# A decoder layer on one Trainium2 core: a fifth seven-product pair in three of the four down-projection passes

## The chip, the core and the metric

The kernel runs on one core of one Trainium2 chip. The core has TensorE (PE, matrix products into PSUM banks of 128 x 512 float32), VectorE (DVE), ScalarE (ACT), GpSimd (POOL) and SyncE (SP, which here only issues DMAs). In the profile PEld is TensorE's weight load. The metric is the device time of one launch in microseconds (us), as the median of the timed runs. Changes within about 0.2% of it cannot be told from no change.

## The reference

One decoder layer: 256 tokens, model width 2048, feed-forward width 5632, all in float32. The part that the change touches is the channel mixer:

```python
h = rmsnorm(x, pre_ffn_g[l])
u = causal_dwconv(h @ w_up[l], conv_w[l], conv_b[l])
gate, val = jnp.split(u, 2, axis=-1)
y = (jax.nn.gelu(gate, approximate=True) * val) @ w_down[l]
x = x + rmsnorm(y, post_ffn_g[l])
```

Ahead of it stand the input projection, two attention groups and the output projection, which stay as they are.

## The kernel before

**Numbers.** A float32 weight tile is split in two parts: ACT copies it to float32r (the high part), DVE subtracts that from the raw values (the low part). A product then is three matmuls: high by high, high by low, low by high (`product`, L963).

**The stages.** The up-projection runs over 22 pairs of 128-channel tiles of gate and value, 11 in each of two halves (`for g`, L1058). For each pair PE makes gate and value, DVE, POOL and ACT do the convolution, the activation and the product, and the result, already transposed, is split into two `G` tiles (channel x token, high and low). After each half the down-projection takes that half's 22 `G` tiles as contraction and runs twice over `w_down`: once for output columns 0 to 1023, once for 1024 to 2047 (`for n in (0, 2)`, L1102). So there are four passes, two per half. Results add up in `y_sb`.

**Eight products or seven.** A pass takes the `G` tiles by pairs `u` (tiles 2u and 2u+1). With the 256 tokens as two blocks, the pair's two tiles as two blocks, and the 1024 columns as two blocks, a pair is a 2x2 block product: eight block products of three matmuls each, 24 matmuls of 512 columns. For the pairs in `FAST` (0, 2, 4, 6) it is done with seven products, 21 matmuls, by sums of blocks: four sums of `G` blocks, made once per half by `token_sums` (L951) and kept split in the tile `sums`, and four differences of weight blocks, made in each pass by DVE (L1007 to L1014) into the tile `tb` and then split like weights. A fast pair thus has ACT and DVE split one 512-column block (`b11`) and three of 1024 (`f13`, `f24`, `b2`), besides the four differences; an ordinary pair splits two of 1024.

**Banks.** Four "early" banks (`m1, m5, m7, m6`, tag "acc") get only products of fast pairs and are summed into `y_sb` after the last fast pair (`add_early`); four "late" banks (`p2, p3, p4, p22`, tag "att") get the rest of the fast pairs and all ordinary products, and are summed after the pass's last pair (L1144 to L1149). The last pair's products are held and done bank by bank (`block`), so that each late bank can leave while PE fills the next. In the last pass three pairs are held, and the end of the kernel (L1170 on) interleaves their four blocks with the final norm.

**Places.** Raw weights, 1024 columns at a time (512 KB), are loaded by SP into eight rotating places: five `raw` tiles, two in `extra`, one in `tb`. Split weights have five pairs of places (`whi`, `wlo`); the last pass keeps its last pair's splits in `rest`. A place is loaded or written again once its last reader is through.

**Order.** PE's instructions stand in the order in which they are written. The other engines' are ordered by a scheduler, which takes a ready instruction by its place in the program; at the end of the kernel, from L1179, they too stand as written. In the first pass of a half the pairs run 1, 3, 0, 5, 2, 7, 4, 8, 6, 9, 10, in the second from 0 to 10.

## Time and profile before

| | |
|---|---|
| timed runs | 1065.41, 1064.84, 1065.19 us; median 1065.19 us |
| profiled execution | 1064.31 us, of which the span of its instructions is 1062.6 us |
| DVE busy in the span | 839.7 us |
| ACT, POOL busy in the span | 639.1 us, 229.3 us |
| DMA read and written | 201.68 MB, 4.21 MB |
| the four passes begin (first matmul) | 580.42, 637.5, 936.94, 994.06 us |

A row of a group names line, engine, operation and tiles, then shapes; "x" is the count. In a table by windows the columns are the window, its length, the busy time (and count) of PE, PEld, DVE, ACT and POOL, the granted TensorE clock, the DMA share and GB/s. A row of a timeline begins with start and duration; in brackets stands the idle time before it and what ended it. A line of waits names who waited for whom: total us, times, longest. Durations overlap: a matmul's row is longer than its distance to the next.

### The profile page before, as it was taken

The page shows a single profiled execution, that of the slowest core. Times are in us where ns is not written, and L with a number is a line of the kernel's source. Part 1 is how long each engine was busy: PE and PEld are TensorE (multiplying, and loading weights), DVE is VectorE, ACT ScalarE, POOL GpSimd, SP SyncE. Part 2 cuts the span into 40 slices and gives each one's busy share as a digit, 9 for nine tenths or more (in the row PEclk, how much of TensorE's full clock was granted, in tenths as well). Part 3 has the DMA queues.
Part 4 walks back from the last instruction along what each step waited for, and adds up shares of the span by engine and source line. Part 5 has one row for each costly group of instructions (what it writes and reads, how often), then busy time and mean ns, then how long its engine had stood idle before and what let it go on. Part 6 is the DMA issues. An engine that isn't in the chain of part 4 may idle for free.

```text
span 1062.6 us, 16272 instructions
## 1 busy us (share of the span) xinstructions
PE 1049.6 (99%) x5890; PEld 914.6 (86%) x5890; DVE 839.7 (79%) x1369; ACT 639.1 (60%) x1096; POOL 229.3 (22%) x256
## 2 busy tenths in 40 slices
PE   9999999999999999999999999999999999999996
PEld 7889988888889888888888888888888888888885
DVE  5988887887467887787767999668778687789987
ACT  6767667776556765566655556446556565556551
POOL 4253335441022121211212000002121121200004
PEclk9999999999999999999999999999999999999998
DMA  8745566555773876656665666666566665656563
GB/s 280 217 120 168 162 209 202 165 170 162 282 236 107 280 231 187 193 180 185 211 188 188 193 204 206 213 196 190 169 209 188 197 197 180 194 179 200 194 242 121
DMA packets 154285, 207.08 MB, mean 195 GB/s; under 512 B 6845, under 2 KB 131037, under 8 KB 153181
## 3 DMA queue, kind: packets, MB, share of 16 engines
q1 hardware_dynamic: 153200, 203.37, 60.7%
q10 hardware_dynamic: 1004, 2.68, 0.6%
q8 instruction: 46, 0.75, 0.3%
q14 instruction: 35, 0.28, 0.1%
HBM read 201.68 MB, written 4.21 MB: 194 GB/s over the span
## 4 chain that ended last, share of the span: by engine, by line
PE 84%; DVE 9%; issue 2%; DMA 2%; ACT 2%; POOL 1%; DVEq 0%; SPq 0%; POOLq 0%; ACTq 0%
PE bank_acc L284 15%; PE bank_att L284 14%; PE bank_acc L309 12%; PE bank_att L967 9%; PE bank_acc L290 8%; PE bank_att L290 7%; PE bank_acc L253 7%; DVE wlo L313 4%; PE bank_acc L258 4%; PE bank_acc L967 2%; PE bank_att L475 1%; PE bank_att L510 1%; DVE wlo L115 1%; PE bank_acc L932 1%; DMA raw<-in_w_down_dram 1%
## 5 line engine op out<-in xcount | busy, mean ns | idle before, releaser
L115 DVE TENSOR_TENSOR wlo<-raw,whi 128x1024 fp32r<-128x1024 f32 (+3 forms) x271 | 328.5, 1224 | 127.0 <-ACT whi L112 118.4
L112 ACT CAST whi<-raw 128x1024 fp32r<-128x1024 f32 (+3 forms) x270 | 273.2, 1029 | 131.8 <-issue 88.8
L899 POOL TENSOR_TENSOR room<-room,rowf 128x256 f32<-128x256 f32 x88 | 100.3, 1160 | 393.9 <-DVE room L898 392.0
L284 PE MATMUL bank_acc<-hT,whi 128*128 128x512 f32 x736 | 173.3, 390 | 0.0
L284 PEld LDWEIGHTS bank_acc<-hT,whi 128*128 128x128 f32 x736 | 136.4, 188 | 27.4
L967 PE MATMUL bank_att<-whi,G 128*128 128x512 f32 x488 | 156.0, 389 | 0.0
L284 PE MATMUL bank_att<-hT,whi 128*128 128x512 f32 x640 | 150.6, 390 | 0.0
L284 PEld LDWEIGHTS bank_att<-hT,whi 128*128 128x128 f32 x640 | 118.7, 188 | 23.9
L967 PEld LDWEIGHTS bank_att<-whi,G 128*128 128x128 f32 x488 | 91.6, 188 | 18.9
L967 PE MATMUL bank_att<-wlo,G 128*128 128x512 f32 x244 | 95.0, 389 | 0.2 <-DVE wlo L313 0.2
L290 PEld LDWEIGHTS bank_acc<-hT,wlo 128*128 128x128 f32 x736 | 89.3, 188 | 2.0
L290 PE MATMUL bank_acc<-hT,wlo 128*128 128x256 f32 x736 | 89.8, 279 | 0.0
L901 ACT ACTIVATE room<-room,cw 128x256 f32<-128x256 f32 x88 | 53.0, 602 | 60.6 <-POOL room L899 60.6
L253 PE MATMUL bank_acc<-hT,whi 128*128 128x512 f32 x352 | 88.0, 395 | 0.0
L309 PE MATMUL bank_acc<-whi,oT 128*128 128x512 f32 (+1 forms) x272 | 81.7, 379 | 0.0
L290 PEld LDWEIGHTS bank_att<-hT,wlo 128*128 128x128 f32 x640 | 77.6, 188 | 1.7
L290 PE MATMUL bank_att<-hT,wlo 128*128 128x256 f32 x640 | 77.9, 279 | 0.0
L903 DVE SCALAR_TENSOR_TENSOR room<-room,cw 128x256 f32<-128x256 f32 x88 | 62.4, 709 | 17.6 <-ACT room L901 17.3
L253 PEld LDWEIGHTS bank_acc<-hT,whi 128*128 128x128 f32 x352 | 63.3, 188 | 11.5
L313 DVE TENSOR_TENSOR wlo<-raw,whi 128x1024 fp32r<-128x1024 f32 (+1 forms) x56 | 61.3, 1119 | 12.1 <-ACT whi L312 12.1
L312 ACT CAST whi<-tb 128x1024 fp32r<-128x1024 f32 x42 | 44.0, 1050 | 43.0 <-PE bank_att L967 19.6
L312 ACT CAST whi<-raw 128x1024 fp32r<-128x1024 f32 (+1 forms) x56 | 52.3, 958 | 27.1 <-PE bank_att L967 20.6
(254 smaller groups left out, 1594.0 us busy)
## 6 DMA issues: line engine op xcount, KB each, us to landing
raw<-in_w_up_dram SPq DMA_DIRECT2D x176, 512.0 KB, 4.2
raw<-in_w_down_dram SPq DMA_DIRECT2D x58, 512.0 KB, 4.7
raw<-in_w_in_dram SPq DMA_DIRECT2D x51, 512.0 KB, 4.7
raw<-in_w_out_dram SPq DMA_DIRECT2D x32, 512.0 KB, 4.6
extra<-in_w_down_dram SPq DMA_DIRECT2D x20, 512.0 KB, 4.7
raw<-in_w_in_dram SPq DMA_DIRECT2D x16, 384.0 KB, 3.6
tb<-in_w_down_dram SPq DMA_DIRECT2D x10, 512.0 KB, 3.5
cb<-c_dram SPq DMA_DIRECT2D x8, 256.0 KB, 3.8
```

Source lines behind the costliest of these rows:

```text
L112: i1 = act.copy(hi[:, cs], raw[:, cs])
L115: i2 = dve.tensor_tensor(lo[:, cs], raw[:, cs], hi[:, cs].bitcast(F32), op=ALU.subtract)
L253: pe.matmul(b, parts[u][0][:, a, m * P:(m + 1) * P], hT[:, kt, :], start=(kt == 0), stop=(kt == KT - 1))
L284: pe.matmul(b, parts[u][0][:, a, m * P:(m + 1) * P], hT[:, kt, :], start=(kt == 0), stop=(kt == KT - 1))
L290: pe.matmul(b[:, 256:512], parts[u][1][:, a, m * P:(m + 1) * P], hT[:, kt, 0:256], start=False, stop=False)
L309: pe.matmul(b, a, r[:, cols], start=(first and i == 0), stop=(last and i == 2))
L312: act.copy(hi, src)
L313: dve.tensor_tensor(lo, src, hi.bitcast(F32), op=ALU.subtract)
L899: pool.tensor_tensor(u[:, 2:258], u[:, 2:258], rowf, op=ALU.mult)
L901: act.activation(y, u[:, 2:258], AF.Identity, bias=cw[:, 3, ch:ch + 1], scale=cw[:, 2, ch:ch + 1])
L903: dve.scalar_tensor_tensor(y, u[:, 1:257], cw[:, 1, ch:ch + 1], y, op0=ALU.mult, op1=ALU.add)
L967: pe.matmul(b[:, to] if to else b, a, r[:, cols], start=(first and i == 0), stop=(last and i == 2))
```

## The change

`FAST` gets pair 8. Three of the four passes use all five pairs; the last pass of the second half keeps four. The first pass of a half runs the pairs in the order 1, 3, 0, 5, 2, 7, 4, 6, 9, 8, 10.

`token_sums` keeps three sums for pairs 0 to 6: the fourth (the sum of the blocks a21 and a22) is written over a21 in the activations before they are split into `G`, where nothing else reads a21. Pair 8 keeps four sums, since it is ordinary in the last pass.

The differences of weight blocks are written over the raw weight tiles, in place of `tb`. Raw tiles have six rotating places in the first half (five `raw`, one `extra`) and eight in the second (two more in the memory of `hT`, free after the last up-projection). Split weights have seven rotating places: the five before, two more in the memory of the convolution's room and a tile `slot`. `rest` is gone. The post-norm's gain table lies in the memory of `hT`.

`fast_pass` becomes `column_pass`, which returns three functions: `ahead` (load and split the first pair), `run` and `block`. The second pass's first pair is prepared before the first pass's last sums are written down, and the pair behind the last fast one before the early sums. In a fast pair the seven products are ordered by when their splits are made; in a pass's first fast pair those into late banks come last.

```diff
-FAST = (0, 2, 4, 6)
+FAST = (0, 2, 4, 6, 8)
...
+        def sums_at(i):
+
+            return (i * 768, 3) if i < 4 else (4 * 768, 4)
+
-        def token_sums(into, y0, y1):
+        def token_sums(i, g, sums, y0, y1):
 
             s = fp.tile([P, 4, P], F32, tag="cst", name="s")
+            at, n = sums_at(i)
             a11, a21 = y0[:, 0:P], y0[:, P:256]
             a12, a22 = y1[:, 0:P], y1[:, P:256]
...
+            if n == 4:
+                split(g[0][:, 0:256], g[0][:, 256:512], y0)
+            split(g[1][:, 0:256], g[1][:, 256:512], y1)
+            dve.tensor_tensor(s[:, 0, :], a11, a21, op=ALU.subtract)
+            s1 = s[:, 3, :] if n == 4 else a21
+            dve.tensor_tensor(s1, a21, a22, op=ALU.add)
+            dve.tensor_tensor(s[:, 1, :], s1, a11, op=ALU.subtract)
+            dve.tensor_tensor(s[:, 2, :], a12, s[:, 1, :], op=ALU.subtract)
+            if n == 3:
+                split(g[0][:, 0:256], g[0][:, 256:512], y0)
+            w = n * P
+            split(sums[:, at:at + w], sums[:, at + w:at + 2 * w],
+                  s[:, 0:n, :].rearrange("p k c -> p (k c)"))
...
-        def fast_pass(G, sums, order, k00, c0, load, tb, early, late, add_early, hold=1,
-                      keep=None):
+        def column_pass(G, sums, some, order, k00, c0, load, parts, hold=1):
...
+            def prepare(u):
+                ra, rb = (load(w_rows(w_down, k00 + 2 * u + a, 1, c0, UNIT)) for a in range(2))
+                if u not in some:
+                    return [parts(r, UNIT) for r in (ra, rb)]
+                b11 = parts(ra[:, left], 512)
+                b2 = parts(rb, UNIT)
+                dve.tensor_tensor(ra[:, left], ra[:, right], ra[:, left], op=ALU.subtract)
+                dve.tensor_tensor(ra[:, right], rb[:, right], ra[:, right], op=ALU.subtract)
+                f13 = parts(ra, UNIT)
+                dve.tensor_tensor(rb[:, right], rb[:, right], ra[:, left], op=ALU.subtract)
+                dve.tensor_tensor(rb[:, left], rb[:, left], rb[:, right], op=ALU.subtract)
+                return b11, b2, f13, parts(rb, UNIT)
+
+            def ahead():
+                ready[order[0]] = prepare(order[0])
...
+                steps = [(m1, of(k, 0), b11, left), (p2, of(k + 1, 0), b2, left),
+                         (p3, s_of(2), b2, right), (m5, s_of(3), f13, left),
+                         (m7, s_of(0), f13, right), (m6, s_of(1), f24, right),
+                         (p4, of(k + 1, 1), f24, left)]
+                if u == fast[0]:
+                    steps = steps[0:1] + steps[3:] + steps[1:3]
+                for bk, a, b, cols in steps:
+                    product(bk, *a, b, cols, first(bk), end and bk in (m1, m5, m7, m6))
+
+            def run(add_early):
+                early, late = ([bank(tag) for _ in range(4)] for tag in ("acc", "att"))
+                banks.extend(zip(late, (0, 0, 1, 1), (left, right, left, right)))
+                for i, u in enumerate(order):
+                    forms = ready.pop(u) if u in ready else prepare(u)
+                    if u in some:
+                        seven(u, forms, *early, *late[:3])
+                        if u == fast[-1] and hold == 1:
+                            nxt = order[i + 1]
+                            ready[nxt] = prepare(nxt)
+                            add_early(*early)
...
-            extra = fp.tile([P, 2, UNIT], F32, tag="gbc", name="extra")
-            tb = fp.tile([P, 3, UNIT], F32, tag="room", name="tb")
-            spare = [extra[:, 0, :], extra[:, 1, :], tb[:, 2, :]]
...
+            extra = fp.tile([P, UNIT], F32, tag="extra", name="extra")
+            raws, units = [extra], [0, 0]
+            if half:
+                more = main.tile([P, 2, UNIT], F32, tag="hT", name="more")
+                raws += [more[:, i, :] for i in range(2)]
+            slots = fp.tile([P, ROOM], F32R, tag="room", name="slots")
+            slots = [slots[:, 544 + i * UNIT:544 + (i + 1) * UNIT] for i in range(3)]
+            slots.append(fp.tile([P, UNIT], F32R, tag="slot", name="slot"))
 
             def load(src):
...
+                i = units[0] % (5 + len(raws)) - 5
...
+            def parts(src, n):
+                i = units[1] % 7 - 5
...
+            passes = [column_pass(G, sums, some, order, half * FHALF, n * 512, load, parts, hold)
+                      for n, some, order, hold in
+                      ((0, FAST, (1, 3, 0, 5, 2, 7, 4, 6, 9, 8, 10), 1),
+                       (2, FAST[:4] if half else FAST, range(FHALF // 2), HOLD if half else 1))]
+            for n, (_, run, block) in zip((0, 2), passes):
+                late = run(early_sums(n))
+                if n == 0:
+                    passes[1][0]()
+                elif half:
...
-        gbf = fp.tile([P, D], F32, tag="gbc", name="gbc_ffn")
+        gbf = main.tile([P, D], F32, tag="hT", name="gbc_ffn")
```

154 lines of the change are left out of this document (56 added, 98 removed).

## The prediction

> **What bounds the kernel now.** I call the four runs over `w_down` passes A and B (first half of the contraction, output columns 0 to 1023 and 1024 to 2047) and C and D (second half, the same columns), and a pair of 128-row tiles "fast" if it runs as seven products. I read the page's first two parts, then what TensorE waited for, then the busy time by stage. The profiled execution took 1064.31 us for a span of 1062.6; the three timed runs have a median of 1065.19. All sums below are differences against the profiled execution, and I add the total to the median.
>
> ```profile
> span 1062.6 us, 16272 instructions
> PE 1049.6 (99%) x5890; PEld 914.6 (86%) x5890; DVE 839.7 (79%) x1369; ACT 639.1 (60%) x1096; POOL 229.3 (22%) x256
> PE bank_acc L169 <- DVE junk L164: 1.3, 1, 1.3
> PE bank_att L522 <- DVE pl L313: 0.5, 1, 0.5
> PE bank_acc L334 <- DMA x_in<-in_x_dram: 0.4, 1, 0.4
> PE bank_att L967 <- DVE wlo L313: 0.2, 1, 0.2
> 580.40:637.50 57.10, 57.10 (x254) 47.28 (x253) 53.96 (x70) 31.11 (x37) 1.79 (x2) 1.00 0.60 198
> 637.50:694.60 57.10, 57.10 (x254) 47.28 (x253) 44.37 (x48) 30.00 (x32) 0.20 (x4) 1.00 0.65 210
> 936.00:993.00 57.00, 57.00 (x253) 47.18 (x252) 53.65 (x69) 31.82 (x39) 1.79 (x2) 1.00 0.61 200
> 993.00:1047.00 54.00, 53.83 (x238) 44.23 (x237) 47.78 (x57) 29.05 (x38) 5.95 (x5) 1.00 0.52 186
> ```
>
> TensorE (PE) is busy 99% of the span at a full granted clock in these stages, and all its waits come to 2.4 us, only 0.2 of it in the passes. In A, B and C it never pauses. VectorE (DVE) is busy 53.96 of 57.10 us in A, 53.65 of 57.00 in C, 44.37 in B. So PE sets the time, and what leaves its list shortens the kernel by its own length, as long as DVE, which is close behind in A and C, stays in front.
>
> ```profile
> 670.86 23.80 PE bank_att L967 x105
> 694.66 3.63 PE bank_acc L284 x16
> 936.94 0.39 PE L967 MATMUL bank_att<-whi,G 128*128 128x512 f32 x1
> 994.06 0.39 PE L967 MATMUL bank_acc<-whi,G 128*128 128x512 f32 x1
> 996.78 0.39 PE L967 MATMUL bank_att<-whi,G 128*128 128x512 f32 x1
> ```
>
> The first row is a run of 105 matmuls of 512 columns in 23.80 us: 0.2267 us each (a matmul's own 0.389 overlaps the next one). C begins at 936.94 and D at 994.06: 57.12 us, the 252 matmuls of seven ordinary pairs (24 each) and four fast ones (21 each) at 0.2267. The row at 996.78 is product `p4` of D's first pair, 12 matmuls after 994.06, the first that writes a bank which C's late sums must have left.
>
> **The change part by part.** (1) *The fifth fast pair.* In A, B and C pair 8 issues 21 matmuls for 24: 3 x 3 x 0.2267 = **2.04 us** less PE work, if nothing else ends later. A pass becomes 249 x 0.2267 = 56.44 us. In D the four pairs stay.
>
> (2) *What it costs DVE.* A fast pair needs five operations of 512 (one low half, four differences) and three low halves of 1024; an ordinary one two of 1024.
>
> ```profile
> 943.21 0.69 DVE L1007 TENSOR_TENSOR tb<-raw 128x512 f32<-128x512 f32 x1
> 943.82 0.68 DVE L1008 TENSOR_TENSOR tb<-extra,raw 128x512 f32<-128x512 f32 x1
> 950.51 1.22 DVE L313 TENSOR_TENSOR wlo<-extra,whi 128x1024 fp32r<-128x1024 f32 x1
> 951.64 1.22 DVE L313 TENSOR_TENSOR wlo<-tb,whi 128x1024 fp32r<-128x1024 f32 x1
> 952.78 0.68 DVE L313 TENSOR_TENSOR wlo<-raw,whi 128x512 fp32r<-128x512 f32 x1
> 586.52 0.69 DVE L1007 TENSOR_TENSOR tb<-raw 128x512 f32<-128x512 f32 x1
> 943.20:972.50 29.30, 29.30 (x131) 24.26 (x130) 29.09 (x34) 17.77 (x19) 0.00 (x0) 1.00 0.62 201
> ```
>
> From start to start these rows give 0.605 us for 512 and 1.137 for 1024, less than their durations. A fast pair is 5 x 0.605 + 3 x 1.137 = 6.44 us of DVE against 4.76 of PE; an ordinary one 2.27 against 5.44. One more fast pair in a pass is 4.17 us more DVE and 0.68 less PE. The last row shows how well DVE runs when loaded: 34 operations (19 of 512, 15 of 1024) are 28.55 us at these paces, and the stretch is 29.3: 0.7 us lost, 2.5%.
>
> Now the deadline. DVE is free of the convolution's tail at 943.21 in C (586.52 in A), with pairs 1 and 3 and pair 0's first low half split. In C it must then do: the rest of pair 0 (5.83), pairs 2, 4, 6, 8 (25.74), pairs 5, 7, 9, 10 (9.10), D's first pair, which the change puts ahead of the late sums (6.44), eight early sums (4.84) and three late ones (1.82), since `p4` of the next pass writes the third late bank: 53.77 us, to 996.98. The new `p4` is due at 936.94 + 56.44 + 2.72 = 996.10. **In C PE waits 0.9 us**, or 0.9 + 2.5% of 53.77 = 2.2 if DVE loses as much as in the row above. I take the middle, **+1.5**. In A there are four early sums on DVE (the first half only stores them): 51.35 us from 586.52, to 637.87 or 639.2 with the loss; `p4` is due at 580.42 + 59.16 = 639.58. No wait in A, by 0.4 to 1.7 us. Before B ends, and in D behind that first wait, an ordinary and a fast pair together are 8.71 of DVE to 10.2 of PE, so DVE gains 1.5 us each time. Bounds of this term: 0 (nothing lost elsewhere, the last early sum put behind the late ones) and +3.2 (the 2.35 us that DVE idles in C today, on loads and ACT, stay: 0.9 + 2.35).
>
> ```profile
> 972.95 1.23 DVE L313 TENSOR_TENSOR wlo<-tb,whi 128x1024 fp32r<-128x1024 f32 x1 [0.47 <-ACT whi L312]
> 975.48 0.69 DVE L1007 TENSOR_TENSOR tb<-extra 128x512 f32<-128x512 f32 x1 [1.31 <-DMA extra<-in_w_down_dram]
> 977.88 0.69 DVE L1008 TENSOR_TENSOR tb<-tb,extra 128x512 f32<-128x512 f32 x1 [0.57 <-DMA tb<-in_w_down_dram]
> ```
>
> Behind a DVE instruction that waits stand all later splits and sums, and PE waits for them once the lead is used up. ACT, busy 31.11 of 57.10 us in A and 31.82 in C, gets 1.4 us more a pass and stays hidden.
>
> (3) *Differences over the raw weights, fewer load places.* The same four operations, written elsewhere: 0. But a raw tile is now held until its pair's last split, and the first half has six load places instead of eight.
>
> ```profile
> DMA to landing us min/median/max: 3.6/4.7/6.2
> ```
>
> Six places are three pairs: the loads of pair 6 (eighth in A) go out when pair 2 (fifth) is done, 20.6 us into A by the sum above, land 4.7 later (two of them by 27), and are wanted when DVE is through with pair 4, at 29.3. The others have 3 us or more. I take 0; the bound above is a rival below. C and D keep eight.
>
> (4) *Seven places for split weights instead of five.* PE never waits for them today, so at best it is what makes (2) possible: a fast pair takes four, and with seven each place is left by PE before DVE wants it (pair 4's last is wanted at 28.4 us into the pass, its predecessor's products end at 24.5). Value 0. The room tile that now holds three of them is next written by the following half's convolution, 11 us after the pass.
>
> (5) *Sums beside the convolution.* Pair 8 adds four operations of 128 columns and a split of 512 in each half, the other four pairs lose a quarter of their split: 0, hidden by the up-projection on PE.
>
> ```profile
> 560.00:580.40 20.40, 20.40 (x122) 18.11 (x121) 15.08 (x22) 11.30 (x18) 4.01 (x4) 1.00 0.61 193
> L313 DVE TENSOR_TENSOR sums<-s,sums x8: 683/685/687, 372.7 to 858.5; 128x512 fp32r<-128x512 f32 x8
> ```
>
> There PE is busy all of 20.40 us and DVE 15.08, so that 5 us are free in the time of one pair's up-projection. Without that cover it would cost at most 4 x 0.605 + 0.68 = 3.1 us of DVE a half.
>
> (6) *The end.* D keeps its products, but its order of splits and its gain table move.
>
> ```profile
> 1026.48 1.05 ACT L312 CAST rest<-raw 128x1024 fp32r<-128x1024 f32 x1 [3.24 <-DMA raw<-in_w_down_dram]
> 1027.56 1.22 DVE L313 TENSOR_TENSOR rest<-raw,rest 128x1024 fp32r<-128x1024 f32 x1 [3.06 <-ACT rest L312]
> 1036.12 1.22 DVE L313 TENSOR_TENSOR wlo<-raw,whi 128x1024 fp32r<-128x1024 f32 x1
> 1032.22 0.33 SPq L1184 DMA_DIRECT2D gbc_ffn<-in_post_ffn_g_dram  x1
> 1040.68 3.00 POOL L1154 TENSOR_TENSOR y_sb<-y_sb,gbc_ffn 128x512 f32<-128x512 f32 x2 [100.80 <-DMA gbc_ffn<-in_post_ffn_g_dram]
> 1043.51 0.39 PE L967 MATMUL bank_att<-whi,G 128*128 128x512 f32 x1
> 1044.17 0.68 DVE L1087 TENSOR_TENSOR y_sb<-bank_att,y_sb 128x512 f32<-128x512 f32 x1
> 1045.71 0.81 DVE L1167 SCALAR_TENSOR_TENSOR rv<-ysq,rv 128x1 f32<-128x1 f32 x1 [0.85 <-ACT junk L1088]
> 1054.79 0.16 DVE L1167 SCALAR_TENSOR_TENSOR rv<-ysq,rv 128x1 f32<-128x1 f32 x1 [0.57 <-ACT junk L1088]
> 1047.18 3.47 DVE L1173 SCALAR_TENSOR_TENSOR y_sb<-y_sb,ry,x_back 128x512 f32<-128x512 f32 x2 [0.66 <-POOL ry L1169]
> 1051.17 1.40 DVE L1173 SCALAR_TENSOR_TENSOR y_sb<-y_sb,ry,x_back 128x512 f32<-128x512 f32 x2
> ```
>
> Today ACT sits 3.24 us for the load of the last pair (tile `rest`) with the splits of pairs 7 to 9 queued behind it, and DVE 3.06. With seven rotating places the last pair's splits come last, so DVE should get to its early sums some 3 us sooner. That is worth little: PE's second block ends at 1043.51, its sum starts at 1044.17 (0.6 late), and the following small operation takes 0.81 beside POOL's gains, 0.16 where POOL is idle; **-1.2** if both go. Against it: the gain table lies in `hT` and waits for pair 8's second load, not its first: one split (1.1 us) and about 1.1 of queue later, with POOL's gains, `ry` and the two 1.7 us operations at 1047.18 behind: **+1.8** at most. The removed wait is the larger of the two in the rows, so I take **-0.6**.
>
> [...]
>
> Sum: -2.04 + 1.5 - 0.6 = **-1.1 us**: 1063.2 by the profiled execution, **1064.0** beside the median.
>
> **The rivals.** *DVE keeps up everywhere:* no wait in C, and the end is 0.6 to 1.2 better: -2.6 to -3.2, about **1062.2**. For it: the sum misses its deadline by only 0.9 us, and DVE's idle time in A and C today is partly that of running too far ahead. Against: the busy shares of A and C. *DVE is the bound:* today's idle time stays in both halves: +3.2 in C and, with the same 2.35 us lost in A, 51.35 + 2.35 against 53.06 = +0.6 there, end unchanged: -2.04 + 3.8, **1067.0**. *The load ring:* slower. With six places a pair's loads leave only when the third pair before it is done, so landing plus splitting must fit three pairs of PE, 15.4 us; splitting a fast pair is 6.4 us of DVE and two ACT steps, about 8.5; it decides from a landing of 6.9 us. At 7.5 each pair of A and B loses 0.2 us, 22 pairs 4.4: -1.1 + 4.4, **1068.5**. Against: a median landing of 4.7 and a longest of 6.2. *Nothing of it:* the scheduler, which orders all engines but PE, could still put late sums ahead of D's first pair; then pair 0 is late instead, the same wait, so this has no time of its own.
>
> [...] A pace at the full durations is a rival of its own: 40 operations of 512 and 26 of 1024 at 0.685 and 1.22 are 59.1 us for C (+6.2) and 56.4 for A (+3.3), so **1073**; the start-to-start rows leave it 1 in 100.
>
> **How the numbers follow.** Forecast (one wait in C of 0.9 to 2.2, end between -1.2 and 0, so 1063.1 to 1065.3) 0.47; DVE keeps up 0.32; DVE the bound 0.12; load ring 0.08; full durations 0.01. About 0.2%, or 2.1 us, is what a measurement of this kernel can tell from no change. The forecast lies wholly within it; DVE keeping up is faster; of DVE the bound a tenth is slower, the last two are. So faster 0.32, same 0.58, slower 0.10. The range takes in the forecast, most of the second case and the third: 1061.8 to 1067.2.
>
> **What the profile will show.** PE should count 5890 - 9 = 5881 matmuls, with 56.4 us each in A and B and no pause there; a pause of about 1.5 us, released by DVE, near 995 in C to D; DVE busy near 100% from 943 to there; a load of `extra` or `raw` that DVE waits for in A means the ring; an earlier first gain on POOL, by about 1 us against D's start, the end. I am wrong if PE waits in A or B, if it waits nowhere, or if the last matmul to the end of the span (1052.1 to 1062.6 today) is not shorter by about 0.6.
>
> ```profile
> 1051.19 0.88 PE L967 MATMUL bank_acc<-rest,G 128*128 128x256 f32 x6
> ```

## The result and the profile after

| | time, us (median; lowest to highest; runs) | ratio to the kernel before [95% interval] | profiled execution / its span, us |
|---|---|---|---|
| before, on the same chip | 1064.98; 1064.28 to 1065.41; 6 | | 1064.31 / 1062.6 |
| the changed kernel | 1073.59; 1072.02 to 1074.44; 6 | 1.0081 [1.0068, 1.0094] | 1074.44 / 1072.7 |

It is 8.6 us, or 0.8%, slower. The forecast was 1.1 faster, and its range ended at 1067.2. The times of the two profiled executions differ by 10.13 us, the spans by 10.1, so the profile shows somewhat more than the medians.

The first lines of the page, what TensorE waited for in the passes, and the busy time of the four passes, each from its first matmul (the columns are those of before):

```profile
span 1072.7 us, 16296 instructions
PE 1051.4 (98%) x5881; PEld 911.4 (85%) x5881; DVE 856.7 (80%) x1397; ACT 642.6 (60%) x1104; POOL 228.0 (21%) x256
PE bank_acc L980 <- DVE slot L313: 4.5, 4, 1.3
PE bank_acc L980 <- DVE wlo L313: 1.9, 3, 0.8
579.60:639.40 59.80, 57.35 (x251) 46.59 (x249) 56.05 (x72) 32.07 (x39) 1.78 (x2) 1.00 0.55 177
639.40:697.80 58.40, 57.03 (x251) 46.68 (x250) 52.42 (x59) 31.48 (x34) 0.20 (x4) 1.00 0.71 228
940.20:999.70 59.50, 57.39 (x251) 46.61 (x250) 56.09 (x72) 31.58 (x39) 1.78 (x2) 1.00 0.59 193
999.70:1063.00 63.30, 60.67 (x271) 48.91 (x269) 54.71 (x66) 30.80 (x42) 9.36 (x8) 0.97 0.51 172
```

TensorE has the 5881 matmuls that were forecast, nine fewer, and yet a longer busy time, since the row of a matmul that is held up grows (0.50 us instead of 0.39 at 593.41). A to D begin at 579.62, 639.40, 940.22 and 999.67; B ends at 697.78, D at 1062.99. So they took 59.8, 58.4, 59.5 and 63.3 us, where 56.44 were expected of the first three and D took 58.0 before. DVE is the releaser of most of this waiting. It is *not* full in A: 56.05 of 59.80 us.

The waits are easiest to count at the weight loads, because a matmul's row (0.39 us) covers part of the next one's wait. Some of the changed kernel's rows (start, duration, operation; in brackets the idle time ahead and what ended it):

```profile
593.41 0.19 PEld L980 LDWEIGHTS bank_acc<-whi,sums 128*128 128x128 f32 x1 [1.13 <-ACT whi L312]
594.66 0.19 PEld L980 LDWEIGHTS bank_acc<-wlo,sums 128*128 128x128 f32 x1 [1.07 <-DVE wlo L313]
607.49 0.19 PEld L980 LDWEIGHTS bank_acc<-slot,sums 128*128 128x128 f32 x1 [1.41 <-DVE slot L313]
655.02 0.19 PEld L980 LDWEIGHTS bank_acc<-slot,sums 128*128 128x128 f32 x1 [1.60 <-DVE slot L313]
967.80 0.19 PEld L980 LDWEIGHTS bank_acc<-slot,sums 128*128 128x128 f32 x1 [1.35 <-DVE slot L313]
1005.97 0.19 PEld L980 LDWEIGHTS bank_att<-wlo,G 128*128 128x128 f32 x1 [0.87 <-DVE wlo L313]
1017.53 0.19 PEld L980 LDWEIGHTS bank_acc<-slot,sums 128*128 128x128 f32 x1 [1.60 <-DVE slot L313]
```

All such rows of the four passes add up to **13.8 us**, against 0.59 in the kernel before (one row, at 1029.98). Call this the sum of waits. DVE ended ten of these 14 waits, ACT four. The sum comes near the result: 13.8 - 0.6 of new waits, less the 2.04 for nine matmuls, less 0.8 that the end is shorter, is 10.4 us; the spans differ by 10.1. At least ten of the 14 are for `f24`, the last of a pair's four splits, ahead of `m6` (`bank_acc`, with `sums`; so are all the rows shown here but that at 1005.97). They lie in A and B too, where none was forecast.

That the account closes so well is partly luck, for two errors in it cancel. A weight load's row overstates a wait: by the starts of the matmuls, the first one costs 0.87 us (from 592.31 to 593.41, less 0.2267) and not 1.13. And a cost is missing that is no wait. In this execution TensorE's granted clock fell right behind the last of D's waits:

```profile
1018.00:1024.00 6.00, 6.00 (x21) 4.75 (x20) 5.56 (x7) 3.61 (x4) 0.00 (x0) 0.72 0.59 174
```

The kernel before has 1.00 in this stretch and 29 matmuls where these are 21. By the starts of the matmuls the lower clock costs about 1.6 us here (an estimate: nine steps from 1018.57 to 1022.20 take 3.63 us, and 9 x 0.2267 are 2.04). So the sum of waits is a measure for comparing the kernels, not the whole loss.

What DVE and ACT did ahead of the first of the waits, in the changed kernel: two timelines, DVE first, then ACT, of pair 0, A's first fast pair.

```profile
588.25 1.22 DVE L313 TENSOR_TENSOR slots<-extra,slots 128x1024 fp32r<-128x1024 f32 x1 [1.12 <-ACT slots L312]
590.53 0.68 DVE L1006 TENSOR_TENSOR extra<-extra,raw 128x512 f32<-128x512 f32 x1
591.25 0.69 DVE L1007 TENSOR_TENSOR extra<-extra 128x512 f32<-128x512 f32 x1
593.39 1.22 DVE L313 TENSOR_TENSOR wlo<-extra,whi 128x1024 fp32r<-128x1024 f32 x1 [1.45 <-ACT whi L312]
```

```profile
587.17 1.05 ACT L312 CAST slots<-extra 128x1024 fp32r<-128x1024 f32 x1 [0.49 <-DVE G L313]
592.31 1.05 ACT L312 CAST whi<-extra 128x1024 fp32r<-128x1024 f32 x1 [3.14 <-DVE extra L1007]
```

The same pair in the kernel before, on DVE:

```profile
587.74 0.69 DVE L1011 TENSOR_TENSOR tb<-extra,tb 128x512 f32<-128x512 f32 x1
588.46 0.69 DVE L1013 TENSOR_TENSOR tb<-extra,tb 128x512 f32<-128x512 f32 x1
589.06 2.50 DVE L313 TENSOR_TENSOR wlo<-tb,whi 128x1024 fp32r<-128x1024 f32 x2
```

Before, the last two differences (L1011, L1013) ran as soon as the tail of the convolution was over, and two low halves, f13's and f24's, followed at once. Now the target of these differences is the raw tile itself (`extra`), which b2's split must have read first. That split goes to `slots`, memory of the convolution's room, free only at 587.17; DVE sits 1.12 us for its high half; the differences (L1006, L1007) come at 590.53 and 591.25, ACT has waited 3.14 us for them, and f24's low half is made at 593.39. TensorE wanted the high half at 592.3 and has idled 1.13 and 1.07 us by 594.66.

### The profile page after: what moved, and what is told of

It reads as the page before. It is cut to its first block, busy times and chain, and to the rows that moved or that the text cites. A ratio compares the mean times of both kernels' runs of the same rounds, so it can differ in the third digit from the quotient of the medians.

```text
span 1072.7 us, 16296 instructions
## 1 busy us (share of the span) xinstructions
PE 1051.4 (98%) x5881; PEld 911.4 (85%) x5881; DVE 856.7 (80%) x1397; ACT 642.6 (60%) x1104; POOL 228.0 (21%) x256
## 4 chain that ended last, share of the span: by engine, by line
PE 79%; DVE 12%; issue 4%; ACT 2%; DMA 1%; POOL 1%; SPq 0%; DVEq 0%; POOLq 0%; ACTq 0%
PE bank_acc L284 15%; PE bank_att L284 14%; PE bank_acc L309 12%; PE bank_acc L290 8%; PE bank_att L290 7%; PE bank_acc L253 7%; PE bank_att L980 6%; PE bank_acc L258 4%; DVE wlo L313 3%; PE bank_acc L980 2%; DVE slot L313 1%; PE bank_att L475 1%; DVE slots L313 1%; PE bank_att L510 1%; DVE wlo L115 1%
## 5 line engine op out<-in xcount | busy, mean ns | idle before, releaser
L980 PE MATMUL bank_att<-whi,G 128*128 128x512 f32 x366 | 120.9, 393 | 0.0
L312 ACT CAST whi<-raw 128x1024 fp32r<-128x1024 f32 (+1 forms) x68 | 63.7, 966 | 34.4 <-DVE raw L1004 15.9
L313 DVE TENSOR_TENSOR wlo<-raw,whi 128x1024 fp32r<-128x1024 f32 (+1 forms) x68 | 74.8, 1129 | 9.8 <-ACT whi L312 9.5
L980 PEld LDWEIGHTS bank_att<-whi,G 128*128 128x128 f32 x366 | 69.4, 190 | 14.8
L253 PEld LDWEIGHTS bank_acc<-hT,whi 128*128 128x128 f32 x352 | 63.3, 188 | 11.5
L980 PE MATMUL bank_att<-wlo,G 128*128 128x512 f32 x183 | 72.0, 394 | 0.4 <-DVE wlo L313 0.4
L309 PEld LDWEIGHTS bank_acc<-whi,oT 128*128 128x128 f32 x272 | 50.2, 188 | 9.3
```

Source lines behind the costliest of these rows:

```text
L253: pe.matmul(b, parts[u][0][:, a, m * P:(m + 1) * P], hT[:, kt, :], start=(kt == 0), stop=(kt == KT - 1))
L309: pe.matmul(b, a, r[:, cols], start=(first and i == 0), stop=(last and i == 2))
L312: act.copy(hi, src)
L313: dve.tensor_tensor(lo, src, hi.bitcast(F32), op=ALU.subtract)
L980: pe.matmul(b[:, to] if to else b, a, r[:, cols], start=(first and i == 0), stop=(last and i == 2))
```

## The experiments

Each kernel has a run of the kernel before beside it on the same chip; ratios are to that. Times are medians. All differences are under 2%, and those of e2, e5, e6, e7, e14 and e15 are within the 0.2% or so that was named at the start; the intervals of e2 and e15 hold 1, those of the other four just don't.

| kernel | us | before beside it | ratio [95% interval] | sum of waits in the passes, us |
|---|---|---|---|---|
| e1 changed kernel, four pairs | 1069.35 | 1064.16 | 1.0047 [1.0032, 1.0062] | 7.2 |
| e2 before, five pairs in A, B, C | 1063.85 | 1064.16 | 0.9996 [0.9986, 1.0006] | 2.6 |
| e3 before, overwriting | 1067.71 | 1064.16 | 1.0030 [1.0018, 1.0042] | 4.7 |
| e4 changed kernel, no heads ahead | 1077.69 | 1064.16 | 1.0120 [1.0105, 1.0135] | 16.0 |
| e5 before, five pairs in A, B | 1062.57 | 1064.09 | 0.9984 [0.9975, 0.9993] | 1.0 |
| e6 changed kernel, own tiles | 1062.96 | 1064.09 | 0.9988 [0.9980, 0.9997] | 3.0 |
| e7 before, f13's differences overwrite | 1065.12 | 1064.09 | 1.0011 [1.0002, 1.0020] | 2.2 |
| e8 before, b2 split first | 1067.31 | 1064.09 | 1.0026 [1.0015, 1.0037] | 4.7 |
| e9 changed kernel, own tiles in C, D | 1067.53 | 1063.88 | 1.0033 [1.0021, 1.0045] | 8.1 |
| e10 e6, overwriting | 1071.56 | 1063.88 | 1.0070 [1.0056, 1.0083] | 11.5 |
| e11 e6, four pairs in C | 1061.26 | 1063.88 | 0.9973 [0.9963, 0.9983] | 0 |
| e12 changed kernel, b2 later | 1081.45 | 1063.88 | 1.0163 [1.0149, 1.0177] | 17.8 |
| e13 e6, f13's differences overwrite | 1069.04 | 1063.88 | 1.0047 [1.0032, 1.0062] | 9.9 |
| e14 e6, f24's differences overwrite | 1065.76 | 1063.88 | 1.0014 [1.0005, 1.0024] | 5.9 |
| e15 e6, six load places in A, B | 1064.59 | 1063.88 | 1.0005 [0.9995, 1.0014] | 5.2 |

The theories at the start: **LOAD**, that a fifth fast pair is more than DVE can do (the prediction's second term, mis-sized), and **CHAIN**, that writing differences over raw weights ties them to the other splits of their pair, so that they come late.

### Is it the fifth pair? (e1, e2, e5)

e1 takes the fifth pair back from the changed kernel and leaves the rest. e2 does the reverse: the kernel before, with its own tile `tb` for the differences and its eight load places, gets the fifth pair in A, B and C, with the sums as changed.

```diff
 e1, against the changed kernel
-FAST = (0, 2, 4, 6, 8)
+FAST = (0, 2, 4, 6)
...
-                      ((0, FAST, (1, 3, 0, 5, 2, 7, 4, 6, 9, 8, 10), 1),
+                      ((0, FAST, (1, 3, 0, 5, 2, 7, 4, 8, 6, 9, 10), 1),
```

```diff
 e2, against the kernel before
-FAST = (0, 2, 4, 6)
+FAST = (0, 2, 4, 6, 8)
...
-                if u in FAST:
+                if u in some:
...
-                    order[:9] = [1, 3, 0, 5, 2, 7, 4, 8, 6]
+                    order[:10] = [1, 3, 0, 5, 2, 7, 4, 6, 9, 8]
...
+                                  FAST[:4] if final else FAST)
```

> The changed kernel with only the fifth pair taken back (pairs 0, 2, 4, 6 in all passes, first pass in the old order); places, differences over the raw weights and heads stay as changed. LOAD (DVE's 4.2 us for a fifth pair in A, B, C is the cause): DVE has its slack back, PE waits under 1 us in the passes, 1064 to 1066 us. CHAIN (the differences over raw weights wait for b2's low half and bring DVE and ACT into turns): the waits at the second fast pair of each pass stay, 1068 to 1072 us. PLACES (six load places, rotating split places, heads): also slow, 1067 us or more.

> The kernel before with only the fifth pair added in A, B and C (sums packed as in the change, order 1 3 0 5 2 7 4 6 9 8 10), but differences in their own tile, eight load places, five split places and heads behind the late sums as before. LOAD: slow, 1069 us or more, with PE waiting for DVE at the ends of A and C. CHAIN: 1063 to 1066 us, waits only between C and D. PLACES: about 1063 to 1066 as well.

e1 is still 5.2 us above the kernel before, so that taking the pair back recovers 3.4 of the 8.6; e2 is 0.3 below it, the same within its interval. e2's longest wait at a weight load and its busy time by window, the last window from 940.0 to 997.3:

```profile
993.51 0.19 PEld L980 LDWEIGHTS bank_acc<-wlo,G 128*128 128x128 f32 x1 [1.81 <-DVE wlo L313]
```

```profile
580.00:637.00 57.00, 57.00 (x253) 47.19 (x252) 56.03 (x73) 33.23 (x39) 1.79 (x2) 1.00 0.58 195
940.00:997.30 57.30, 55.85 (x245) 45.36 (x244) 56.67 (x70) 35.42 (x44) 0.00 (x0) 1.00 0.55 184
```

No wait in A (TensorE 57.00 of 57.00), DVE full from 940 to 997 (56.67 of 57.30), and three waits of 2.58 us in all from C into D. That is near the prediction's second term, 0.9 to 2.2 us near 995, bounds 0 and 3.2, though TensorE waits here for low halves of splits and not for a bank. So the fifth pair by itself is not what costs 8.6 us; it adds to the loss only where differences overwrite.

e5 takes C's fifth pair out of e2 again, and with it C's changed order.

```diff
-                    order[:10] = [1, 3, 0, 5, 2, 7, 4, 6, 9, 8]
+                    order[:10] = [1, 3, 0, 5, 2, 7, 4, 8, 6, 9] if half else \
+                        [1, 3, 0, 5, 2, 7, 4, 6, 9, 8]
...
-                                  FAST[:4] if final else FAST)
+                                  FAST[:4] if half else FAST)
```

> The kernel of e2 with its fifth pair in the first half alone, so that the second half is that of the kernel before (own tile for the differences). LOAD SUM (term 2 of the prediction, as e2's trace bore it out: DVE keeps up in A and late in C only): two passes with 9 matmuls fewer, 2 x 9 x 0.2267 = -1.36 us in all with no wait behind it, where e2 had -2.04 + 2.58 of waits: about 1.3 to 1.5 us below the kernel before, some 1062.7 to 1063.0, and weight-load waits in the passes of 0.6 us or less. NOT WORTH IT (what a fifth pair takes from TensorE comes back somewhere that the waits don't show): 1064.0 or above, span within 0.5 us of the span before.

1062.57, 1.5 us below: six matmuls fewer (three in each of A and B) are 6 x 0.2267 = 1.36 us, as the sum has it where DVE keeps up. (The expectation's factor "2 x 9" should be 2 x 3; its result is right.)

### Overwriting in the kernel before (e3, e7, e8)

e3 writes the four differences over the raw tiles, which needs b2's split ahead of them; four pairs, all else as before. e8 only moves b2's split ahead and overwrites nothing. e7 overwrites with f13's two differences only.

```diff
 e3, against the kernel before
+                    b2 = parts(rb, UNIT)
-                    dve.tensor_tensor(t13[:, left], ra[:, right], ra[:, left], op=ALU.subtract)
+                    dve.tensor_tensor(ra[:, left], ra[:, right], ra[:, left], op=ALU.subtract)
...
-                    f24 = parts(t24, UNIT)
-                    b2 = parts(rb, UNIT)
+                    f24 = parts(rb, UNIT)
 e8, against the kernel before
                     b11 = parts(ra[:, left], 512)
+                    b2 = parts(rb, UNIT)
...
                     f24 = parts(t24, UNIT)
-                    b2 = parts(rb, UNIT)
 e7, against the kernel before
-                    t13, t24 = tb[:, 0, :], tb[:, 1, :]
+                    t13, t24 = ra, tb[:, 1, :]
```

> The kernel before, four fast pairs, with only the differences written over the raw weights (b2 split first); all places and heads as before. LOAD: 1064 to 1066 us, no waits. CHAIN: 1068 us or more, PE waiting for a fast pair's last low half. PLACES: 1064 to 1066.

> The kernel before, with four pairs, of which only the first two differences (f13's) are written over the pair's first raw tile; the other two stay in the tile of their own, and b2's split stays behind them in the program. In e3, where both were written over raw weights, the time was +3.5 us. CHAIN THROUGH b2 (the long link is the second raw tile: b2's low half needs a split place, and the other two differences and f24 stand behind it): the short link, b11's low half of 512, costs nothing: 1063.8 to 1065.0, waits in the passes under 1 us. ANY IN-PLACE WRITE (the first raw tile too is held until b11's split): half of e3's loss or more, 1065.8 to 1067.

> The kernel before, with four pairs and its own tiles for the differences, but b2 split ahead of the differences as in e3 and the changed kernel; nothing is overwritten, so the scheduler may still make the differences while b2's split waits for a place. CHAIN (only the overwriting ties the differences to b2): as before, 1063.8 to 1065.0, waits in the passes under 1 us. ORDER (that b2 comes ahead in the program is enough, e3's loss is due to it): 1066.5 to 1068, with waits at D's first pair as in e3.

e3 costs 3.5 us, with waits mostly at D's first pair; two of its weight loads:

```profile
996.13 0.19 PEld L967 LDWEIGHTS bank_acc<-wlo,sums 128*128 128x128 f32 x1 [1.16 <-DVE wlo L313]
999.12 0.19 PEld L967 LDWEIGHTS bank_acc<-wlo,sums 128*128 128x128 f32 x1 [1.07 <-DVE wlo L313]
```

This looked like CHAIN. But e8, which overwrites nothing, costs 3.2 us as well:

```profile
981.32 0.19 PEld L967 LDWEIGHTS bank_acc<-wlo,sums 128*128 128x128 f32 x1 [1.19 <-DVE wlo L313]
999.11 0.19 PEld L967 LDWEIGHTS bank_acc<-wlo,sums 128*128 128x128 f32 x1 [1.70 <-DVE wlo L313]
```

There CHAIN missed. In the kernel before the products take b2 last, so a b2 that is split early probably spends DVE and split places on what TensorE wants last (this reading wasn't tried apart); in any case e3 can't tell order from overwriting. In the changed kernel, though, b2's two products were moved ahead too; so the question had to be put in its own frame. e7's +1.0 us lies between its two expectations, nearer to that of the later link, but its 2.2 us of waits are more than that one allowed; e13 below contradicts the later link.

### Overwriting in the changed kernel's own frame (e6, e10, e9, e13, e14)

e6 keeps the changed kernel's order of splits and products, its heads made ahead, its sums and its five pairs, and gives the differences a tile of their own again; with that come the eight load places and five places for split weights in the first half, seven in the second (two in `hT`). e10 is e6 but for one line.

```diff
 e6, against the changed kernel
-                dve.tensor_tensor(ra[:, left], ra[:, right], ra[:, left], op=ALU.subtract)
+                t13, t24 = tb[:, 0, :], tb[:, 1, :]
+                dve.tensor_tensor(t13[:, left], ra[:, right], ra[:, left], op=ALU.subtract)
...
-            raws, units = [extra], [0, 0]
+            tb = fp.tile([P, 3, UNIT], F32, tag="room", name="tb")
+            slot = fp.tile([P, UNIT], F32, tag="slot", name="slot")
+            raws, units, slots = [extra, slot, tb[:, 2, :]], [0, 0], []
             if half:
...
-                more = main.tile([P, 2, UNIT], F32, tag="hT", name="more")
+                more = main.tile([P, 4, UNIT], F32R, tag="hT", name="more")
+                slots = [more[:, i, :] for i in range(4)]
...
 e10, against e6
-                t13, t24 = tb[:, 0, :], tb[:, 1, :]
+                t13, t24 = ra, rb
```

> The changed kernel in its order, its ahead-of-time heads, its sums and its five pairs in A, B and C, but with the four differences of a pair in a tile of their own and the raw tiles left as loaded; memory as in the kernel before in the first half (eight load places, five places for split weights), seven places for split weights in the second half. CHAIN (in place, b11's and b2's low halves must have read a raw tile before it is overwritten, and these need places that TensorE frees; so the differences can't be made ahead): nearly all 13.8 us of waits go, but for about 0.5 to 2.6 us from C into D, and the three passes' 2.04 us less of TensorE stay: 1062.0 to 1064.0. LOAD (five pairs are too much for DVE in this order): waits in A, B and C stay at 1 to 3 us each, 1067 to 1072. HEADS (the heads put ahead of the late sums disturb): a wait of 1 us or more at each pass's start, 1066 to 1069.

> e6 with one edit: the differences are written over the raw tiles again (the tile of their own is kept and not used), so that memory, places, order and pairs are e6's. It is the changed kernel but for its memory plan (six load places and seven places for split weights in the first half, three of these in the convolution's room). OVERWRITING: most of the 10.6 us between e6 and the changed kernel comes back, 1068 to 1073, with waits at f24 of the second fast pair in A and B and in D's first pairs. PLACES: 1063 to 1065, and the rest is the memory plan's.

e6 takes 1062.96, e10 1071.56: **8.6 us for the one line**, and the sum of waits rises by 8.5. Again not all of it is waiting, for the granted clock is low behind D's waits in e10 too, and nowhere in e6's passes:

```profile
1015.00:1021.00 6.00, 5.56 (x17) 4.47 (x18) 5.13 (x7) 2.94 (x3) 0.00 (x0) 0.72 0.37 121
```

Of e10's four executions, two with a mean clock of 0.997 took 1070.10 and 1070.79 us, two with 0.995 took 1072.33 and 1072.88. Without the lower clock the line costs some 7.5 us. How it happens can be read where A goes over into B. Both kernels run in step there (A begins at 579.47 and 579.78). Pair 0 of B lies in `slot` and `tb`; L1004 to L1008 are its four differences, L313 its low halves. DVE in e6:

```profile
624.28 0.68 DVE L1004 TENSOR_TENSOR tb<-slot 128x512 f32<-128x512 f32 x1
629.69 0.68 DVE L313 TENSOR_TENSOR wlo<-slot,whi 128x512 fp32r<-128x512 f32 x1
630.30 0.68 DVE L1008 TENSOR_TENSOR tb<-tb 128x512 f32<-128x512 f32 x1
636.76 1.21 DVE L313 TENSOR_TENSOR wlo<-tb,whi 128x1024 fp32r<-128x1024 f32 x1
```

ACT in e6, the high half of f24:

```profile
635.50 1.05 ACT L312 CAST whi<-tb 128x1024 fp32r<-128x1024 f32 x1 [3.75 <-PE bank_att L980]
```

DVE in e10, then ACT's high halves of f13 and f24 there, then weight loads:

```profile
630.39 0.68 DVE L313 TENSOR_TENSOR wlo<-slot,whi 128x512 fp32r<-128x512 f32 x1
633.32 0.68 DVE L1004 TENSOR_TENSOR slot<-slot 128x512 f32<-128x512 f32 x1
638.14 0.68 DVE L1008 TENSOR_TENSOR tb<-tb 128x512 f32<-128x512 f32 x1
640.02 1.23 DVE L313 TENSOR_TENSOR wlo<-tb,whi 128x1024 fp32r<-128x1024 f32 x1
```

```profile
635.91 1.06 ACT L312 CAST whi<-slot 128x1024 fp32r<-128x1024 f32 x1 [5.12 <-DVE slot L1005]
638.94 1.05 ACT L312 CAST whi<-tb 128x1024 fp32r<-128x1024 f32 x1 [1.97 <-DVE tb L1008]
```

```profile
640.04 0.19 PEld L980 LDWEIGHTS bank_acc<-whi,sums 128*128 128x128 f32 x1 [0.76 <-ACT whi L312]
641.30 0.19 PEld L980 LDWEIGHTS bank_acc<-wlo,sums 128*128 128x128 f32 x1 [1.07 <-DVE wlo L313]
```

In e6 the first difference runs 5.4 us ahead of b11's low half (624.28, 629.69): it needs only the raw tiles. All four are through at 630.30. What f24's high half waits for is a split place that TensorE must leave (3.75 us, at 635.50), and DVE has used that time; the low half follows at 636.76, and TensorE doesn't stop. In e10 the first difference may not overwrite the raw tile until b11's low half has read it. It comes 2.9 us behind it, between the pass's sums, where the scheduler put it; the last comes at 638.14, 7.8 us later than in e6. Now ACT waits for DVE, 5.12 us for f13's differences and 1.97 for f24's, and f24's low half is 3.3 us later. TensorE loses 3.28 us in four waits there. DVE has no more work than in e6; what it lost is the freedom to do the differences in the time when the split places are full. In A it is even less busy than in e6 (55.91 of 57.00 us):

```profile
579.78:637.00 57.22, 57.22 (x253) 47.11 (x251) 54.61 (x69) 31.94 (x38) 1.79 (x2) 1.00 0.58 188
```

e9 asks the same from the other side: the changed kernel with its memory plan, but own tiles (in `hT`) in C and D alone.

```diff
-                more = main.tile([P, 2, UNIT], F32, tag="hT", name="more")
+                more = main.tile([P, 4, UNIT], F32, tag="hT", name="more")
+                tb = more[:, 2:4, :]
```

> The changed kernel, but in the second half (C and D) the differences are written to a tile of their own in the memory of hT; the first half stays in place, and the seven places for split weights, three of them in the convolution's room, stay in both. In the changed kernel C's waits come to 3.3 us and D's to 4.9. OVERWRITING (what is lost hangs on the differences being tied to the other splits of their pair): C and D fall to the some 3 us that e6 has there, A and B stay as they were: 1067.5 to 1069.5. PLACES (the places for split weights in the room's memory, free only after the convolution's tail, hold the first fast pair up, and the rest follows from that): C's waits at its first fast pair stay, 2 us near 953 to 955, and the total is 1071 or above.

1067.53, 6.1 us below the changed kernel by the medians, about 5 by the two ratios. A and B keep their five waits (5.7 us), C has none, and in D, which begins at 997.04, two are left

```profile
999.58 0.19 PEld L980 LDWEIGHTS bank_acc<-whi,sums 128*128 128x128 f32 x1 [0.77 <-ACT whi L312]
1012.88 0.19 PEld L980 LDWEIGHTS bank_acc<-slot,sums 128*128 128x128 f32 x1 [1.60 <-DVE slot L313]
```

though three of the seven places for split weights still lie in the room's memory. C without overwriting doesn't stop for them. With overwriting they may add something in the first half: e10, which has no such places, has no wait in A (the changed kernel 3.6 us) and 3.3 us in B (2.1); C and D are alike in the two.

Which of the two overwritten tiles is it?

```diff
 e13, against e6
-                t13, t24 = tb[:, 0, :], tb[:, 1, :]
+                t13, t24 = ra, tb[:, 1, :]
 e14, against e6
-                t13, t24 = tb[:, 0, :], tb[:, 1, :]
+                t13, t24 = tb[:, 0, :], rb
```

> e6 with only the first two differences (f13's) written over the first raw tile; the other two stay in the tile of their own. TIE (a difference may start only when the last split that reads its target is done, so that it is no more made ahead; each of the two targets ties two differences, and the two of f24 hang on those of f13 by their data anyway): b11's low half is an early split, so part of e10's 8.6 us, 2 to 5, 1065 to 1068. LATER LINK ONLY (b2's low half is the one that is late): 1063 to 1064, as e7 in the kernel before (+1.0).

> e6 with only the other two differences (f24's) written over the second raw tile, and f13's in the tile of their own. LATER LINK ONLY: nearly all of e10's 8.6 us, 1069 to 1072. TIE: part of it, 1065 to 1068, so that this and e13 share the loss.

Both: +6.1 and +2.8 us on e6, which add up to 8.9, near e10's 8.6. The larger part is the *first* tile's, more than I expected of it. The tie to b11's early low half holds all four differences, as f24's are made from f13's; the tie to b2 holds only the last two. In both, TensorE waits 1.07 us for f24's low half in B's first pair, as in e10.

### The load ring and the order (e15, e4, e12)

e15 is e6 with six load places in the first half.

```diff
-            raws, units, slots = [extra, slot, tb[:, 2, :]], [0, 0], []
+            raws, units, slots = [extra, slot, tb[:, 2, :]][:3 if half else 1], [0, 0], []
```

> e6 with six load places instead of eight in the first half, as the changed kernel has them; differences in their own tile, so that a raw tile is free after its last split or difference, as in e6. LOAD RING (the prediction's rival: with six places loads leave too late for DVE and ACT): waits for a load in A and B and 1 us or more lost in each, 1065 to 1068. NO RING (in the changed kernel's trace DVE waits for no load in A or B): 1062.4 to 1063.8, as e6.

1064.59: 1.6 us above e6, between the two expectations, and for the reason that the load ring gave. DVE waits for a load in A, and TensorE a little later; a DVE row and a weight load of e15:

```profile
602.80 0.69 DVE L1005 TENSOR_TENSOR tb<-raw 128x512 f32<-128x512 f32 x1 [1.87 <-DMA raw<-in_w_down_dram]
607.28 0.19 PEld L980 LDWEIGHTS bank_att<-wlo,G 128*128 128x128 f32 x1 [1.36 <-DVE wlo L313]
```

The DVE row is pair 4's second difference. In the changed kernel this one starts at 608.07, 5.3 us later, and DVE waits for no load in A or B. The ring is real, but its wait is hidden by a worse one. What the memory plan adds beyond overwriting, e10 to the changed kernel, is 1.0070 against 1.0081, about 1 us and within the two intervals; the sum of waits says 2.3 us, all of it in the first half.

e4 takes the heads made ahead out of the changed kernel; e12 puts b2's split, and its products, behind f13's.

```diff
 e4, against the changed kernel
-                if n == 0:
-                    passes[1][0]()
-                elif half:
+                if n and half:
...
 e12, against the changed kernel
                 b11 = parts(ra[:, left], 512)
-                b2 = parts(rb, UNIT)
...
                 f13 = parts(ra, UNIT)
+                b2 = parts(rb, UNIT)
...
+                else:
+                    steps = steps[0:1] + steps[3:5] + steps[1:3] + steps[5:]
```

> The changed kernel without the pass heads made ahead of the late sums (the next pass's first pair is prepared at its turn). LOAD and CHAIN: within 1.5 us of the changed kernel's 1073.6, since the same work only changes its place. PLACES, in the form that the heads ahead hold the late banks back: 1070 us or less.

> The changed kernel with one edit of order: b2 is split behind f13 instead of ahead of the differences (it still stands ahead of the second two differences, which overwrite its source), and its two products stand behind f13's. Products, places and overwriting stay. e8, where b2 ahead cost 3 us with nothing overwritten, asks for it. ORDER (b2's split ahead of f13 and f24 is what comes too late for TensorE): 1066 to 1070, the waits at f24 gone or halved. OVERWRITING (f24 stands behind b2's low half wherever that is written): 1072 to 1076, waits at f24 of 1 us and more in A to D as before.

Both are slower than the changed kernel, by 4.1 us (1.0120 against 1.0081) and 7.9 us (1.0163), and by more than any of their expectations. Their sums of waits are only 2.2 and 4.0 us higher; here too the lower clock adds to it. e4's profiled execution, without it, took 1075.06 us, its three others, at a mean clock of 0.994 to 0.995, 1077.31 to 1078.13; in e12 the clock falls to 0.59 at 644 to 648 and 0.51 at 1012 to 1016 us. A weight load of each, at D's first fast pair, e4 first:

```profile
1005.47 0.19 PEld L980 LDWEIGHTS bank_acc<-whi,sums 128*128 128x128 f32 x1 [2.53 <-ACT whi L312]
```

```profile
1008.62 0.19 PEld L980 LDWEIGHTS bank_acc<-whi,sums 128*128 128x128 f32 x1 [3.61 <-ACT whi L312]
```

So neither the heads nor b2's place is to blame: both help where differences overwrite. The likely reason in e12 is that a b2 split later holds f24 still longer. ORDER, which e8 had suggested, falls for the changed kernel.

### A version that beats both (e11)

e6's waits (1.37 and 1.60 us) lie 3 and 16 us behind D's start, at its first two fast pairs. They can be what C's fifth pair costs DVE, the prediction's second term. e11 gives C four fast pairs.

```diff
-                      ((0, FAST, (1, 3, 0, 5, 2, 7, 4, 6, 9, 8, 10), 1),
+                      ((0, FAST[:4] if half else FAST,
+                        (1, 3, 0, 5, 2, 7, 4, 8, 6, 9, 10) if half else
+                        (1, 3, 0, 5, 2, 7, 4, 6, 9, 8, 10), 1),
```

> e6 with four fast pairs in C as in D, five in A and B only; otherwise the same. LOAD (e6's two waits from C into D, 1.37 and 1.60 us, come of DVE being full from C's start on, as term 2 of the prediction has it): 4.17 us less of DVE in C, the waits go, and TensorE gets back 9 x 0.2267/3 = 0.68: 2.0 to 2.3 us below e6, 1060.6 to 1061.2. HEADS (they come of the order around the head put ahead): 1062.3 to 1063.7, with at least 1.5 us of them left.

1061.26, 1.7 us below e6 (2.0 to 2.3 were expected) and 2.6 below the kernel before. Both waits in D are gone. The windows of A, B and C show no pause:

```profile
580.00:637.00 57.00, 57.00 (x253) 47.16 (x252) 55.91 (x72) 33.10 (x40) 1.79 (x2) 1.00 0.63 202
637.00:694.00 57.00, 57.00 (x253) 47.12 (x252) 51.65 (x60) 31.98 (x34) 0.20 (x4) 1.00 0.66 209
936.00:993.00 57.00, 57.00 (x253) 47.22 (x252) 56.64 (x73) 33.47 (x41) 1.79 (x2) 1.00 0.64 204
```

## Why the prediction was wrong

**The step that failed is (3):** "The same four operations, written elsewhere: 0." The four operations are the same, and so is the row of each, 0.68 to 0.69 us in e6 and in e10; but where they are written sets *when they may run*. In a tile of their own they depend on the loads alone. Over the raw weights they stand behind b11's and b2's low halves, and these behind split places that TensorE frees. The step looked at the other side of the same edit, that a raw tile is held longer, and went on to count loads. e6 against e10 puts a price on it: 8.6 us, of which about 1 is the lower clock. That this is also the loss beside the kernel before is chance: e6 is 1.1 us below that kernel, and about 1 us more is the memory plan's, if it is real. The prediction's own sign of being wrong came true: TensorE waits in A and B, 5.7 us by the sum of waits.

- *(1) 2.04 us less of TensorE:* right. 5881 matmuls; e5 and e11 get the gain of two passes where nothing waits.
- *(2) One wait of 0.9 to 2.2 us from C into D, none in A:* about right for the change that it sums, as e2 shows (2.6 us, none in A or B), if above the 0.9 to 2.2 and not at the bank: in the changed kernel the one wait for a late sum is 0.21 us, at 1003.64. But it was a sum of DVE's work against one deadline at the end of a pass. In the changed kernel each f24 has a deadline of its own, and was late while DVE had 3.75 us to spare in A.
- *(4) Seven places, value 0:* its own value wasn't measured apart. The text did look at when the room is next written, not at when it becomes free: at 587.17 the first b2 waits for it. By e9 that costs nothing in C without overwriting.
- *(5) Sums beside the convolution, 0:* nothing speaks against it; A begins at 579.62, 0.8 us earlier than before.
- *(6) The end, -0.6:* -0.8 (from the last matmul's end to the span's end 9.7 us, 10.5 before), partly for the reason given. No run shows a ground for the other bound that the forecast gives it, 0. The rows of the changed kernel's end, on DVE and then on POOL:

```profile
1048.92 0.69 DVE L1154 TENSOR_TENSOR y_sb<-s,y_sb 128x512 f32<-128x512 f32 x1
1056.18 0.39 DVE L1192 SCALAR_TENSOR_TENSOR rv<-ysq,rv 128x1 f32<-128x1 f32 x1 [0.85 <-ACT junk L1106]
```

```profile
1051.50 5.05 POOL L1179 TENSOR_TENSOR y_sb<-y_sb,gbc_ffn 128x512 f32<-128x512 f32 x4 [108.35 <-DMA gbc_ffn<-in_post_ffn_g_dram]
```

and the last early sum before, on DVE:

```profile
1041.47 1.05 DVE L1130 TENSOR_TENSOR y_sb<-s,y_sb 128x512 f32<-128x512 f32 x1
```

The last early sum starts 14.1 us before TensorE's end (1062.99) instead of 10.6, and the small operation takes 0.39 us instead of 0.81. The gains did not come earlier, as forecast: the first starts 51.8 us behind D's start, 46.6 before, and 11.5 and 11.4 us ahead of TensorE's end.

Of the rivals, *DVE the bound* and *DVE keeps up* both took the differences to be free to move. *The load ring* was the one on the slower side: e15 finds it at about a third of its 4.4 us, but it is not what slowed the changed kernel. *Full durations* gave a time near the result, 1073, by luck, for e2 refutes its mechanism: with 59.1 us of DVE work in C, it would have lost over 6 us there, not 2.6.

Left open: what lowers the clock behind some of the waits; and why the first tile's tie costs only 1.0 us in the kernel before (e7) and 6.1 in e6 (e13). The two differ in order, in the number of pairs and in the heads, and which of these does it wasn't tried apart.

## What to carry to other kernels

Before writing a result over its input to save memory, list who else reads that input and what *they* wait for: the result inherits those waits, and loses the chance to be made in idle time. A sum of an engine's work against the end of a stage says whether the engine keeps up, not whether each consumer gets its piece in time; where a producer runs only a few microseconds ahead, sum up to each consumer's own deadline. When a change frees memory and spends it in the same step, measure the two alone: here the fifth pair was worth 1.5 us in two passes (e5), and the tile given up for it cost 8.6 (e6 against e10).

## What was unexpected of the hardware

A late split is often paid for twice. The first matmul of a product needs the high half, the next the low half, which DVE makes only when ACT has made the high one: in the changed kernel 1.13 us at 593.41 are followed by 1.07 at 594.66, and the second recurs as 1.07 in e1, e3, e4, e10, e12, e13 and e14. It is what DVE's row of 1.22 us leaves, as both start when ACT is done (593.39 and 593.41) and the load itself takes 0.19.

A cluster of waits can cost more than the waits. Behind some of them the granted clock fell, with TensorE at work again: to 0.60 from 1018 to 1022 us in the changed kernel, to 0.62 from 1016 to 1020 in e10, to 0.59 and 0.51 in the stretches of e12 named above. It does not always: e13's profiled execution has the last three waits of e10's D, of the same lengths within 0.01 us, and kept 1.00: its weight loads behind them, from 1014.54 on, start 0.23 us apart, those of e10, from 1017.19 on, at first 0.43.
